# The last feature tile of a down projection, computed in two token ranges

## The chip, the cores and the metric

The kernel runs on one core of one Trainium2 chip. The metric is device time in microseconds (us) of one execution, lower is better. Three runs of the kernel before are known: 1992.32, 1992.97 and 1994.06 us, median 1992.97. Beside them there is a profile of one execution, which gives the start and duration of every instruction on the five engines: TensorE (PE; its weight loads are listed apart as PEld), VectorE (DVE), ScalarE (ACT), GpSimd (POOL) and SyncE (SP), which issues most transfers.

## The reference

One layer of a decoder trunk on 256 prompt tokens and 64 sample tokens (8 sequences of 8), model width 2048, in float32: a gated linear attention beside a causal pooling branch, merged by gates, projected and added to the residual; then a SwiGLU network of inner width 5632; then a last RMS norm. The change touches only the end:

```
gate, up = jnp.split(h2 @ w_gu, 2, axis=-1)
x = x + g2 * ((jax.nn.silu(gate) * up) @ w_down)
...
y_prompt = _rmsnorm(xp, final_norm_g)
y_sample = _rmsnorm(xs, final_norm_g)
```

The norm of a token needs the sum of squares over all 2048 features of that token. Different tokens do not depend on each other there.

## The kernel before

Activations lie with features on the 128 partitions and tokens along the free axis: `x1[k]` is feature tile k (16 tiles of 128 features) with T = 320 columns, 256 prompt tokens (TP) first, then 64 sample tokens (TS). Every large product is made in three passes of a rounded float32 type (fp32r): the weights are split into `hi` (a rounding copy, ScalarE, line 147) and `lo` (the rest, VectorE, line 148), the activations likewise, and `mm3` (lines 160 to 163) adds hi x hi, hi x lo and lo x hi into one PSUM bank. Each of these matmuls is preceded by a load of its 128 x 128 weights, also where two in a row use the same ones.

`proj` (line 165) computes two feature tiles at once. It loads chunks of four rows of weight tiles by 256 columns (512 KB, issued by SyncE, line 139), splits each in pairs, and runs 2 x 3 matmuls of 320 tokens for each of the two feature tiles per pair. `whi` and `wlo` have four buffers each (WB), the raw chunks five in two pools.

The SwiGLU inner width is handled in two halves of 22 tiles (`parts`). For each half the gate and up projections come first, then the down projection of that half over eight units `ui` of two feature tiles, added to `x1` by `residual` (lines 949 to 954). In the second half each finished feature tile k is also squared and added to `acc2` (lines 941 to 947), scaled by the norm's weight into `xg` (line 1052), transposed on TensorE in three pieces of 128 tokens (the helper `tr`, line 125), and copied from PSUM into the row tiles `yn[0..2]` (line 1058), which have tokens on partitions. The third row tile holds the 64 sample tokens alone, padded with zeros in `xg`.

After the last unit, the sums over features are made by matmuls of `acc2` with a column of ones (line 1066), then root and reciprocal (lines 1070 and 1071), and the six halves of the three row tiles are scaled, on VectorE for the first 1024 features (line 1078) and on ScalarE for the others (line 1080), and sent by SyncE (line 1082).

The order of instructions on each engine is written by a planner when the program is built: it runs a timeline of its own, takes whatever is ready in that timeline, and prefers what stands earlier in the program. At run time each engine keeps that order and waits by semaphores. PSUM accumulators come from a pool of two (`pm`), the small ones from a pool of four (`misc()`).

Of the kernel before, what the change touches and what calls it, by code (L numbers as in the profile page):

```python
# [79 lines left out]
def body(tc, A):  # L80
# [17 lines left out]
    def misc():  # L98
        return pmisc.tile([P, 512], F32, tag="m", name=nm("pm"))
# [23 lines left out]
    def tr(out, in_):  # L123
        k = in_.shape[0]
        PE.transpose(out, in_, ident[:k, :k])  # L125
# [815 lines left out]
    def sq_acc(acc, k, first):  # L941
        if first:
            S.activation(acc, x1[k], AF.Square)
        else:
            sq = fp.tile([P, T], F32, tag="sq", bufs=2, name=nm("sq"))
            S.activation(sq, x1[k], AF.Square)
            V.tensor_tensor(acc, acc, sq, op=ALU.add)
# [60 lines left out]


    acc2 = fp.tile([P, T], F32, tag="acc", name="acc2")  # L1010
    parts = ((0, 22), (22, 44))
    for pi, (f0, f1) in enumerate(parts):
        ah, al = {}, {}
# [21 lines left out]
        if pi == 0:  # L1035
            bcx.close()
        else:
            hcx.close()
            yp = ctx.enter_context(tc.tile_pool(name="yp", bufs=1, side="right"))
            yn = [yp.tile([P, D], F32, name="yn%d" % i) for i in range(3)]  # L1040
            xgs = [yp.tile([P, 3 * P], F32, name="xg%d" % i) for i in range(2)]
            for xg in xgs:
                G.memset(xg[:, T:3 * P], 0.0)
        for ui in range(8):
            ps = proj(wdn, 256 * ui, f0, f1, ah, al)
            for i in range(2):
                k = 2 * ui + i
                residual(ps, i, k, 5)
                if pi == 1:
                    sq_acc(acc2, k, k == 0)  # L1050
                    xg = xgs[k % 2]
                    S.activation(xg[:, 0:T], x1[k], AF.Copy, scale=FG[:, k:k + 1])
                    pt = misc()
                    for a in range(3):
                        tr(pt[:, a * P:(a + 1) * P], xg[:, a * P:(a + 1) * P])
                    for a in range(3):
                        n = P if a < 2 else TS
                        (S.copy if a == 0 else V.tensor_copy)(yn[a][:n, k * P:(k + 1) * P], pt[:n, a * P:(a + 1) * P])
            if pi == 1 and ui == 5:
                S.activation(tiny, acc2[:, 0:1], AF.Sqrt)  # L1060


    pt = misc()
    for a in range(3):
        n = P if a < 2 else TS
        PE.matmul(pt[:n, 2 * a:2 * a + 2], lhsT=acc2[:, a * P:a * P + n], rhs=ones[:, 0:2], start=True, stop=True)
    rr = fp.tile([P, 6], F32, name="rr")
    for a in range(3):
        n = P if a < 2 else TS
        S.activation(rr[:n, 2 * a:2 * a + 2], pt[:n, 2 * a:2 * a + 2], AF.Sqrt, scale=1.0 / D, bias=epst[:n])  # L1070
        V.reciprocal(rr[:n, 2 * a:2 * a + 2], rr[:n, 2 * a:2 * a + 2])
    ys = A["y_s"].rearrange("b t d -> (b t) d")
    for a in range(3):
        n = P if a < 2 else TS
        for c in range(2):
            sl = yn[a][:n, c * 1024:(c + 1) * 1024]
            if c == 0:
                V.tensor_scalar(sl, sl, rr[:n, 2 * a:2 * a + 1], None, op0=ALU.mult)
            else:
                S.activation(sl, sl, AF.Copy, scale=rr[:n, 2 * a:2 * a + 1])  # L1080
            dst = A["y_p"][0, a * P:(a + 1) * P] if a < 2 else ys
            nc.sync.dma_start(dst[:, c * 1024:(c + 1) * 1024], sl)
    ctx.close()


# [19 lines left out]
```

## Time and profile before

| what | us |
|---|---|
| median of three runs | 1992.97 (1992.32 to 1994.06) |
| span of the profiled execution, first to last instruction | 1989.4 |
| its last unit of the down projection (1953.6 to 1973.6) | 20.0 |
| from there to the end of the span | 15.8 |
| TensorE busy over the span | 1938.0 (97%) |

The time of an execution is taken around the whole program, the span from its first to its last instruction inside it; the profiled execution's own time is not listed apart from its span, and the median of the runs stands 3.6 us above that span. The page gives the busy time of each engine, 40 slices of the span, the transfers, the chain of work that ended last, and groups of equal instructions by line. Lines are those of the kernel before. A duration in a row is that of one instruction; instructions of one engine overlap in part, so the distance between two starts is the price of one in a stream.

### The profile page before, as it was taken

How to read it: one execution, taken by the hardware profiler on the slowest of the kernel's cores; microseconds unless marked ns; L12 is line 12 of the kernel's file. 1: busy time of each engine (PE TensorE's matmuls, PEld its weight loads, DVE VectorE, ACT ScalarE, POOL GpSimd, SP SyncE). 2: the span in 40 equal slices, each digit the busy share in tenths (PEclk: the TensorE clock that was granted, in tenths of full speed). 3: DMA queues.
4: the chain of work that ended last, by engine and by line, in shares of the span. 5: the costliest groups of instructions: out<-in, count | busy, mean ns of one | idle time of the engine just before them, and what ended most of it. 6: DMA issues, size and time to landing. Idle time of an engine off the chain costs nothing.

```text
span 1989.4 us, 34665 instructions
## 1 busy us (share of the span) xinstructions
PE 1938.0 (97%) x13808; PEld 1819.7 (91%) x13808; DVE 1002.8 (50%) x1918; ACT 829.4 (42%) x1483; POOL 179.3 (9%) x292
## 2 busy tenths in 40 slices
PE   5999999999999999999999999999999999999997
PEld 3778998889999889989979999999999999999997
DVE  2655645656356635665574444444444444444554
ACT  3323633544336433653344333433333434344443
POOL 1002101212121112111130000000000000000000
PEclk9999999999999999999999999999999999999998
DMA  9997458758975888479836555444444444444443
GB/s 316 344 333 239 141 170 281 231 182 288 302 221 171 274 283 257 148 248 329 265 100 197 185 185 178 156 147 145 150 148 154 149 151 151 152 150 140 149 141 101
DMA packets 309276, 400.59 MB, mean 201 GB/s; under 512 B 12418, under 2 KB 273058, under 8 KB 308778
## 3 DMA queue, kind: packets, MB, share of 16 engines
q1 hardware_dynamic: 279754, 291.17, 46.8%
q0 software_dynamic: 29360, 107.21, 15.6%
q8 instruction: 108, 1.77, 0.4%
q14 instruction: 54, 0.43, 0.1%
HBM read 373.90 MB, written 24.67 MB: 200 GB/s over the span
## 4 chain that ended last, share of the span: by engine, by line
PE 90%; DMA 6%; DVE 2%; ACT 1%; issue 0%; SPq 0%; POOL 0%; ACTq 0%; DVEq 0%
PE ps L161 26%; PE ps L163 26%; PE ps L162 26%; PE pm L281 3%; DMA araw<-w_ada 2%; DMA raw<-w_in 2%; PE pm L125 2%; PE pm L221 1%; DMA raw<-w_o 1%; PE pm L767 1%; PE pm L746 1%; PE pm L715 1%; DMA vr<-b_ada 1%; DVE wlo L148 1%; ACT whi L147 0%
## 5 line engine op out<-in xcount | busy, mean ns | idle before, releaser
L148 DVE TENSOR_TENSOR wlo<-raw,whi 128x512 fp32r<-128x512 f32 x952 | 654.9, 692 | 804.8 <-ACT whi L147 801.3
L147 ACT CAST whi<-raw 128x512 fp32r<-128x512 f32 x952 | 586.2, 622 | 923.3 <-PE ps L162 811.2
L161 PE MATMUL ps<-hh,whi 128*128 128x320 f32 x1408 | 443.1, 315 | 4.2 <-ACT whi L147 3.2
L162 PE MATMUL ps<-hl,whi 128*128 128x320 f32 x1408 | 439.2, 312 | 0.0
L163 PE MATMUL ps<-hh,wlo 128*128 128x320 f32 x1408 | 436.6, 312 | 1.3 <-DVE wlo L148 1.3
L161 PE MATMUL ps<-h2h,whi 128*128 128x320 f32 x1408 | 435.7, 310 | 0.0
L162 PE MATMUL ps<-h2l,whi 128*128 128x320 f32 x1408 | 435.5, 309 | 0.0
L163 PE MATMUL ps<-h2h,wlo 128*128 128x320 f32 x1408 | 435.4, 309 | 0.0
L161 PEld LDWEIGHTS ps<-hh,whi 128*128 128x128 f32 x1408 | 264.9, 188 | 28.2 <-issue 16.2
L163 PEld LDWEIGHTS ps<-hh,wlo 128*128 128x128 f32 x1408 | 264.2, 188 | 13.7 <-issue 7.3
L162 PEld LDWEIGHTS ps<-hl,whi 128*128 128x128 f32 x1408 | 265.1, 188 | 5.4 <-issue 4.6
L161 PEld LDWEIGHTS ps<-h2h,whi 128*128 128x128 f32 x1408 | 264.3, 188 | 3.4 <-ACT ah L317 3.4
L162 PEld LDWEIGHTS ps<-h2l,whi 128*128 128x128 f32 x1408 | 264.3, 188 | 0.0
L163 PEld LDWEIGHTS ps<-h2h,wlo 128*128 128x128 f32 x1408 | 264.3, 188 | 0.0
L161 PE MATMUL ps<-ah,whi 128*128 128x320 f32 x704 | 217.7, 309 | 0.0
L162 PE MATMUL ps<-al,whi 128*128 128x320 f32 x704 | 216.5, 308 | 0.0
L163 PE MATMUL ps<-ah,wlo 128*128 128x320 f32 x704 | 216.5, 308 | 0.0
L162 PEld LDWEIGHTS ps<-al,whi 128*128 128x128 f32 x704 | 132.0, 187 | 0.0
L161 PEld LDWEIGHTS ps<-ah,whi 128*128 128x128 f32 x704 | 131.9, 187 | 0.0
L163 PEld LDWEIGHTS ps<-ah,wlo 128*128 128x128 f32 x704 | 131.9, 187 | 0.0
L255 POOL DMA_DIRECT2D araw<-w_ada x64 | 54.9, 862 | 448.5 <-PE pm L281 419.2
L161 PE MATMUL ps<-mh,whi 128*128 128x320 f32 x256 | 79.5, 310 | 0.7 <-ACT whi L147 0.7
(280 smaller groups left out, 1609.4 us busy)
## 6 DMA issues: line engine op xcount, KB each, us to landing
raw<-w_gu SPq DMA_DIRECT2D x176, 512.0 KB, 3.5
raw<-w_in SPq DMA_DIRECT2D x173, 512.0 KB, 4.5
araw<-w_ada POOLq DMA_DIRECT2D x64, 1024.0 KB, 8.5
raw<-w_down SPq DMA_DIRECT2D x80, 512.0 KB, 3.5
raw<-w_ada SPq DMA_DIRECT2D x64, 512.0 KB, 6.6
S<-state_gla POOLq DMA_DIRECT2D x16, 1024.0 KB, 9.6
o_gs<-S POOLq DMA_DIRECT2D x16, 1024.0 KB, 5.9
raw<-w_o SPq DMA_DIRECT2D x32, 512.0 KB, 5.1
```

What stands on the lines that cost most here:

```text
L125: PE.transpose(out, in_, ident[:k, :k])
L147: S.copy(hi, raw)
L148: V.tensor_sub(lo, raw, hi.bitcast(F32))
L161: PE.matmul(ps, lhsT=whi, rhs=xhi, start=start, stop=False)
L162: PE.matmul(ps, lhsT=whi, rhs=xlo, start=False, stop=False)
L163: last_mm[:] = [PE.matmul(ps, lhsT=wlo, rhs=xhi, start=False, stop=stop).ins]
L221: PE.matmul(ps[32 * j:32 * j + 32, 0:w], lhsT=scT[:, k0 + i, :], rhs=raw[:, i, :], start=r == 0, stop=r == 3, tile_position=(0, 32 * j))
L255: nc.gpsimd.dma_start(t[:, r:r + step], wada[:, k0 + r:k0 + r + step, col:col + nb * P])
L281: PE.matmul(ps[32 * j:32 * j + 32, 0:w], lhsT=scT[:, k0 + r + j, :], rhs=ada_raw[n][:, r + j, :], start=k0 == 0 and first, stop=k0 + nk == ...
L715: PE.matmul(pt, lhsT=E["kdn"][:, s, d * P:(d + 1) * P], rhs=E["vn"][:, s], start=s == 0, stop=s == 1)
L746: PE.matmul(pt[32 * j:32 * j + 32, :], lhsT=qeP[:, d, 4 * gg + j, :], rhs=E["S0", gg, d][:, j], start=False, stop=d == 0, tile_position=(0 ...
L767: PE.matmul(pt, lhsT=E["kpn"][:, j, d * P:(d + 1) * P], rhs=E["vp"][:, gg], start=True, stop=True)
```

## The change

The last unit (feature tiles 14 and 15) is taken out of the loop for the second half. Its weights are loaded as before. Tile 14 is computed over all 320 tokens, while the split weights of tile 15 are kept in two new tiles (`wlast`, hi and lo). Tile 15 is then computed twice with them: for tokens 0 to 191, and for tokens 192 to 319 (TC = 192) in another PSUM tile. After each range its residual, squares, transposes and copies follow, and then `rows`, which makes the norms of that range's tokens, scales their rows and sends them.

The three windows of 128 tokens for transposes start at 0, 64 and 192 (WIN) and no longer at 0, 128 and 256; the middle one overlaps the first, and of it only its second half is sent. The third holds the last 64 prompt tokens and the 64 sample tokens. So there are eight output transfers, two of 128 rows and six of 64, where there were four of 128 rows and two of 64. The three row tiles become one tile, with one copy from PSUM per feature tile, on VectorE for even k and on ScalarE for odd k. The zero padding of `xg` goes.

```diff
 
 
     acc2 = fp.tile([P, T], F32, tag="acc", name="acc2")
+    TC = 192
+    WIN = (0, TC - P, TC)
+
+    def residual_part(acc, k, t0, t1):
+        e = min(t1, TP)
+        V.scalar_tensor_tensor(x1[k][:, t0:e], acc[:, t0:e], modp(5, k), x1[k][:, t0:e], op0=ALU.mult, op1=ALU.add)
+        if t1 > TP:
+            t = fp.tile([P, TS], F32, tag="rt", bufs=2, name=nm("rt"))
+            V.tensor_tensor(s3(t), s3(acc[:, TP:T]), mods(5, k), op=ALU.mult)
+            V.tensor_tensor(x1[k][:, TP:T], x1[k][:, TP:T], t, op=ALU.add)
+
+    def finish(k, t0, t1):
+
+        if k == 0:
+            S.activation(acc2, x1[k], AF.Square)
+        else:
+            sq = fp.tile([P, T], F32, tag="sq", bufs=2, name=nm("sq"))
+            S.activation(sq[:, t0:t1], x1[k][:, t0:t1], AF.Square)
+            V.tensor_tensor(acc2[:, t0:t1], acc2[:, t0:t1], sq[:, t0:t1], op=ALU.add)
+        xg = xgs[k % 2]
+        if t0 == 0:
+            S.activation(xg[:, t0:t1], x1[k][:, t0:t1], AF.Copy, scale=FG[:, k:k + 1])
+        else:
+            V.tensor_scalar(xg[:, t0:t1], x1[k][:, t0:t1], FG[:, k:k + 1], None, op0=ALU.mult)
+        pt = misc()
+        wins = [a for a in range(3) if t0 <= (TC if a == 2 else 0) and WIN[a] + P <= t1]
+        for a in wins:
+            tr(pt[:, a * P:(a + 1) * P], xg[:, WIN[a]:WIN[a] + P])
+        a, b = wins[0], wins[-1] + 1
+        (S.copy if k % 2 else V.tensor_copy)(yn[:, a:b, k * P:(k + 1) * P],
+                                             pt[:, a * P:b * P].rearrange("p (a t) -> p a t", t=P))
+
+    rr = fp.tile([P, 3, 2], F32, name="rr")
+    ys = A["y_s"].rearrange("b t d -> (b t) d")
+    yrows = ((A["y_p"][0, 0:P], 0, P, 0), (A["y_p"][0, P:TC], P - (TC - P), P, 1),
+             (A["y_p"][0, TC:TP], 0, TP - TC, 2), (ys, TP - TC, P, 2))
+
+    def rows(t0, t1):
+
+        a0, a1 = (0, 2) if t0 == 0 else (2, 3)
+        pt = misc()
+        for a in range(a0, a1):
+            PE.matmul(pt[:, 2 * a:2 * a + 2], lhsT=acc2[:, WIN[a]:WIN[a] + P], rhs=ones[:, 0:2], start=True, stop=True)
+        r = rr[:, a0:a1]
+        S.activation(r, pt[:, 2 * a0:2 * a1].rearrange("p (a t) -> p a t", t=2), AF.Sqrt, scale=1.0 / D, bias=epst)
+        V.reciprocal(r, r)
+        for a in range(a0, a1):
+            for c in range(2):
+                sl = yn[:, a, c * 1024:(c + 1) * 1024]
+                if c == 0:
+                    V.tensor_scalar(sl, sl, rr[:, a, 0:1], None, op0=ALU.mult)
+                else:
+                    S.activation(sl, sl, AF.Copy, scale=rr[:, a, 0:1])
+                for dst, p0, p1, aa in yrows:
+                    if aa == a:
+                        nc.sync.dma_start(dst[:, c * 1024:(c + 1) * 1024], yn[p0:p1, a, c * 1024:(c + 1) * 1024])
+
     parts = ((0, 22), (22, 44))
     for pi, (f0, f1) in enumerate(parts):
         ah, al = {}, {}
@@ -1037,49 +1094,51 @@
         else:
             hcx.close()
             yp = ctx.enter_context(tc.tile_pool(name="yp", bufs=1, side="right"))
-            yn = [yp.tile([P, D], F32, name="yn%d" % i) for i in range(3)]
-            xgs = [yp.tile([P, 3 * P], F32, name="xg%d" % i) for i in range(2)]
-            for xg in xgs:
-                G.memset(xg[:, T:3 * P], 0.0)
+            yn = yp.tile([P, 3, D], F32, name="yn")
+            xgs = [yp.tile([P, T], F32, name="xg%d" % i) for i in range(2)]
+            wlast = [yp.tile([P, f1 - f0, P], F32R, name="wlast%d" % i) for i in range(2)]
         for ui in range(8):
+            if pi == 1 and ui == 7:
+                break
             ps = proj(wdn, 256 * ui, f0, f1, ah, al)
             for i in range(2):
                 k = 2 * ui + i
                 residual(ps, i, k, 5)
                 if pi == 1:
-                    sq_acc(acc2, k, k == 0)
-                    xg = xgs[k % 2]
-                    S.activation(xg[:, 0:T], x1[k], AF.Copy, scale=FG[:, k:k + 1])
-                    pt = misc()
-                    for a in range(3):
-                        tr(pt[:, a * P:(a + 1) * P], xg[:, a * P:(a + 1) * P])
-                    for a in range(3):
-                        n = P if a < 2 else TS
-                        (S.copy if a == 0 else V.tensor_copy)(yn[a][:n, k * P:(k + 1) * P], pt[:n, a * P:(a + 1) * P])
+                    finish(k, 0, T)
             if pi == 1 and ui == 5:
                 S.activation(tiny, acc2[:, 0:1], AF.Sqrt)
 
-
-    pt = misc()
-    for a in range(3):
-        n = P if a < 2 else TS
-        PE.matmul(pt[:n, 2 * a:2 * a + 2], lhsT=acc2[:, a * P:a * P + n], rhs=ones[:, 0:2], start=True, stop=True)
-    rr = fp.tile([P, 6], F32, name="rr")
-    for a in range(3):
-        n = P if a < 2 else TS
-        S.activation(rr[:n, 2 * a:2 * a + 2], pt[:n, 2 * a:2 * a + 2], AF.Sqrt, scale=1.0 / D, bias=epst[:n])
-        V.reciprocal(rr[:n, 2 * a:2 * a + 2], rr[:n, 2 * a:2 * a + 2])
-    ys = A["y_s"].rearrange("b t d -> (b t) d")
-    for a in range(3):
-        n = P if a < 2 else TS
-        for c in range(2):
-            sl = yn[a][:n, c * 1024:(c + 1) * 1024]
-            if c == 0:
-                V.tensor_scalar(sl, sl, rr[:n, 2 * a:2 * a + 1], None, op0=ALU.mult)
-            else:
-                S.activation(sl, sl, AF.Copy, scale=rr[:n, 2 * a:2 * a + 1])
-            dst = A["y_p"][0, a * P:(a + 1) * P] if a < 2 else ys
-            nc.sync.dma_start(dst[:, c * 1024:(c + 1) * 1024], sl)
+    f0, f1 = parts[1]
+    ps = pmain.tile([P, 2, 512], F32, tag="pm", name=nm("ps"))
+    psb = pmain.tile([P, 2, 512], F32, tag="pm", name=nm("ps"))
+    wh, wl = wlast
+    for c0 in range(f0, f1, 4):
+        nk = min(4, f1 - c0)
+        raw = raw_chunk(wdn[:, c0:c0 + nk, 256 * 7:256 * 8], nk, 256)
+        for j in range(0, nk, 2):
+            hi = wp.tile([P, 2, 256], F32R, tag="whi", bufs=WB, name=nm("whi"))
+            lo = wp.tile([P, 2, 256], F32R, tag="wlo", bufs=WB, name=nm("wlo"))
+            src = raw[:, j:j + 2, 0:P]
+            S.copy(hi[:, :, 0:P], src)
+            V.tensor_sub(lo[:, :, 0:P], src, hi[:, :, 0:P].bitcast(F32))
+            q = c0 - f0 + j
+            src = raw[:, j:j + 2, P:2 * P]
+            S.copy(wh[:, q:q + 2], src)
+            V.tensor_sub(wl[:, q:q + 2], src, wh[:, q:q + 2].bitcast(F32))
+            for n in range(2):
+                kt = c0 + j + n
+                mm3(ps[:, 0, :T], hi[:, n, 0:P], lo[:, n, 0:P], ah[kt], al[kt], kt == f0, kt == f1 - 1)
+    residual(ps, 0, KT - 2, 5)
+    finish(KT - 2, 0, T)
+    for t0, t1 in ((0, TC), (TC, T)):
+        acc = ps[:, 1] if t0 == 0 else psb[:, 0]
+        for kt in range(f0, f1):
+            q = kt - f0
+            mm3(acc[:, t0:t1], wh[:, q], wl[:, q], ah[kt][:, t0:t1], al[kt][:, t0:t1], kt == f0, kt == f1 - 1)
+        residual_part(acc, KT - 1, t0, t1)
+        finish(KT - 1, t0, t1)
+        rows(t0, t1)
     ctx.close()
 
 
```

## The prediction

> **What bounds the kernel now.** I read the page first, then the last 36 us in two windows, then single instructions of the tail, and last the transfers.
>
> ```profile
> span 1989.4 us, 34665 instructions
> PE 1938.0 (97%) x13808; PEld 1819.7 (91%) x13808; DVE 1002.8 (50%) x1918; ACT 829.4 (42%) x1483; POOL 179.3 (9%) x292
> PE 90%; DMA 6%; DVE 2%; ACT 1%; issue 0%; SPq 0%; POOL 0%; ACTq 0%; DVEq 0%
> core 0: us, PE busy (x) PEld busy (x) DVE busy (x) ACT busy (x) POOL busy (x), PEclk, DMA share, GB/s
> 1953.60:1973.60 20.00, 20.00 (x139) 19.77 (x137) 8.71 (x20) 6.95 (x14) 0.00 (x0) 1.00 0.05 14
> 1973.60:1989.40 15.80, 1.69 (x13) 1.30 (x12) 5.70 (x18) 5.87 (x12) 0.00 (x0) 0.67 0.49 166
> ```
>
> TensorE is busy for 97% of the span and carries 90% of the chain that ended last. The first window is the last unit of the down projection (feature tiles 14 and 15): TensorE without a gap, at granted clock 1.00, VectorE under half busy, hardly a DMA. The second is the tail, 15.8 us in which TensorE works 1.69. The change shortens the second window and pays in the first, so two prices decide: a matmul of fewer tokens, and what the tail becomes.
>
> The tail in order (start, duration, engine, line):
>
> ```profile
> 1973.05 0.31 PE L161 MATMUL ps<-ah,whi 128*128 128x320 f32 x1
> 1973.34 0.30 PE L163 MATMUL ps<-ah,wlo 128*128 128x320 f32 x1
> 1973.68 0.48 DVE L950 SCALAR_TENSOR_TENSOR x<-ps,mod,x 128x256 f32<-128x256 f32 x1 [5.84 <-PE ps L163]
> 1974.08 0.21 DVE L953 TENSOR_TENSOR rt<-ps,mod 128x64 f32<-128x64 f32 x1
> 1977.90 0.55 ACT L1070 ACTIVATE rr<-pm,epst 128x2 f32<-128x2 f32 x3 [0.28 <-PE pm L1066]
> 1978.35 0.17 DVE L1071 RECIPROCAL rr<-rr 128x2 f32<-128x2 f32 x1
> 1978.43 0.73 DVE L1078 TENSOR_SCALAR yn<-yn,rr 128x1024 f32<-128x1024 f32 x1
> 1979.24 0.36 SPq L1082 DMA_DIRECT2D y_p<-yn  x1
> ```
>
> The last matmul starts at 1973.34, the first output transfer is issued at 1979.24 (5.90 us later), and the span ends at 1989.4: 16.06 us after that last start. Two matmul starts 0.29 apart over two steps give 0.147 us per matmul of 320 tokens. The remaining 10 us are transfers:
>
> ```profile
> GB/s 0 0 0 0 0 0 14 410 423 382 423 410 423 341 423 396 410 410 423 396 382 423 437 355 301 273 232 205 219 218 205 205 0 0 0 0 0 0 0 27
> y_p<-yn SPq DMA_DIRECT2D x4, 512.0 KB, 4.4
> y_s<-yn SPq DMA_DIRECT2D x2, 256.0 KB, 4.8
> 1980.10:1981.40 1.30, 0.00 (x0) 0.00 (x0) 0.45 (x1) 1.30 (x2) 0.00 (x0) 0.50 1.02 406
> ```
>
> The first row has 40 slices of 0.3 us from 1978.0. Data flow from 1980.10, 0.86 after the first issue; the four 128-row pieces run at about 405 GB/s, and once only 64-row pieces of y_s are left (the slices from 232 to the last 205) the rate is 214. Check: 2.1 MB at 405 and 0.52 MB at 214 take 5.18 + 2.45 = 7.63, so data end near 1987.73, and 1.67 us close the span.
>
> **The change part by part.** *Feature tile 15 in two ranges.* 66 matmuls of 320 tokens become 66 of 192 and 66 of 128. Every matmul still loads its own 128 weight columns, so the floor of that load counts:
>
> ```profile
> 810.03 0.23 PE L580 MATMUL pm<-cumr,w 128*128 128x128 f32 x1
> 810.09 0.27 PE L581 MATMUL pm<-cumr,w 128*128 128x128 f32 x1
> 810.03 0.30 PEld L581 LDWEIGHTS pm<-cumr,w 128*128 128x128 f32 x2
> 1977.05 0.53 PEld L1066 LDWEIGHTS pm<-cst,acc 128*128 128x128 f32 x4
> L163 PEld LDWEIGHTS ps<-hh,wlo 128*128 128x128 f32 x1408 | 264.2, 188 | 13.7 <-issue 7.3
> ```
>
> L580 and L581 are the only fp32r matmuls here with few moving columns. The 128-column one streams in 0.06 (810.03 to 810.09), so 0.46 ns per column as at 320; 192 would stream in 0.09. But weight loads follow one another no faster than 0.11: two span 0.30, one lasts 0.19; four span 0.53, (0.53 - 0.19)/3 = 0.113, there under matmuls of two columns. At 320 tokens that load hides under 0.147; at 192 and 128 it does not. I take 0.110 for both: 132 x 0.110 = 14.52 against 66 x 0.147 = 9.70, **+4.82 us**. Bounds: +0.1 if only streaming counted (66 x (0.09 + 0.06) = 9.9, with rounding 0.1 to 0.2 over the old), +5.2 at 0.113.
>
> [...]
>
> *Transposes and row sums inside the stream.* Three transposes of tile 14 and two of the first range, and four weight loads of its row sums, stood in the tail.
>
> ```profile
> 1959.48 0.31 PE L163 MATMUL ps<-ah,wlo 128*128 128x320 f32 x1
> 1959.62 0.49 PE L125 MATMUL pm<-cst,xg 128*128 128x128 f32 x3
> 1960.10 0.31 PE L162 MATMUL ps<-al,whi 128*128 128x320 f32 x1
> 1956.17 0.55 ACT L1052 ACTIVATE xg<-x,vec 128x320 f32<-128x320 f32 x1
> ```
>
> From 1959.48 to 1960.10 go two matmuls and three transposes: (0.62 - 0.29)/3 = 0.11 each. So 9 x 0.11 = **+0.99**. Queued behind them on TensorE are the second range's matmuls; they would wait if the inputs were late, but here xg is ready at 1956.72 and the transposes stand 2.9 us later in the order, so I cost that wait at nothing.
>
> *Tile 14 alone, splits for both.* TensorE now spends 0.88 per pair of rows of weights where it spent 1.76, while the same raw chunk is split into hi, lo and the kept weights of tile 15.
>
> ```profile
> L148 DVE TENSOR_TENSOR wlo<-raw,whi 128x512 fp32r<-128x512 f32 x93 | 64.3, 692 | 71.5 <-ACT whi L147 71.5
> L947 DVE TENSOR_TENSOR acc<-acc,sq 128x320 f32<-128x320 f32 x15 | 7.3, 490 | 1.8 <-ACT sq L946 1.2
> L946 ACT ACTIVATE sq<-x 128x320 f32<-128x320 f32 x15 | 6.9, 463 | 7.9 <-DVE x L954 7.9
> L1058 DVE COPY yn<-pm 128x128 f32<-128x128 f32 x16 | 4.7, 291 | 3.7 <-ACT yn L1058 3.6
> L1058 ACT COPY yn<-pm 128x128 f32<-128x128 f32 x16 | 4.2, 265 | 8.2 <-PE pm L125 8.2
> L1070 ACT ACTIVATE rr<-pm,epst 128x2 f32<-128x2 f32 x2 | 0.4, 260 | 0.3 <-PE pm L1066 0.3
> ACT whi L147 <- PE ps L162: 5.6, 5, 1.1
> 1955.43 0.37 SPq L139 DMA_DIRECT2D raw<-w_down  x1
> ```
>
> VectorE per pair: between 0.69 (one 512-wide operation) and 2 x 0.49 (320-wide rows). Eleven pairs are 7.6 to 10.8, plus 2 x (0.48 + 0.21 + 0.21 + 0.49) and a copy, some 3.3, for tiles 12 and 13, in 10.0 us of TensorE and with three pairs split ahead (ScalarE's cast waits for TensorE to free its buffers), worth 2.6. Stall: 0 to 1.5; I take 0, as two 256-wide halves lie nearer the one 512-wide row. The last raw transfer is issued 1.8 us into the unit, so loads are ahead. One 384-wide copy of output rows for three narrow ones, and the dropped zero fill on GpSimd, lie under TensorE's stream: nothing. Without that cover the copies count 0.27 + 2 x 0.29 now and at most some 0.5 (the 320-wide rows) then.
>
> *Rows of the first range during the second.* The second range holds TensorE 66 x 0.110 + 6 x 0.11 = 7.9 us. In it: residual (under 0.48), square (0.46), sum (0.49), row sums (0.7), root and reciprocal (0.26 + 0.17), scaling 0.73, with hand-overs: first issue 3.7 us after the first range ends, or 6.6 with the 2.9 us of lateness seen above. Its 128-row pieces (1.05 MB) need 2.6, its 64-row pieces (0.52 MB) 2.45. With 0.86 to the first data they end at 9.6 to 12.5, that is 1.7 to 4.6 us after the second range's last matmul.
>
> *What is left of the tail.* From the last matmul start: 0.30 to VectorE, three 64-wide operations 0.64, square at most 0.27, sum at most 0.29, row sums 0.5 (two loads and a matmul), root 0.26, reciprocal 0.17, scaling 0.73, issue 0.08: first issue at 3.24, data at 4.10. What they wait behind is at worst the first range's pieces until 4.6. Then 1.05 MB, now all in pieces of 64 rows, at 214 GB/s: 4.9; close 1.67. Sum 10.67 against 16.06: **-5.39**. Bounds: -7.8 if pieces of opposite partition halves shared the rate of 405 (2.6 for 4.9, less 0.1 for the second issue), -4.4 with 0.5 of waiting for the first range and 0.5 of longer hand-overs.
>
> [...]
>
> Sum: 4.82 + 0.99 + 0 - 5.39 = **+0.4 us**, 1989.8 against the span of 1989.4. The median of the runs, 1992.97, lies 3.6 above that span (launch and end outside it), which I keep: 1993.4.
>
> **The rivals.**
>
> *The weight load hides after all.* In a long stream of short matmuls the loads would overlap and streaming would set the pace. For it: the 0.06 between the two 128-column matmuls. Against: the loads around them stand 0.11 apart, and the four under two-column matmuls do too. Price: -4.7, so 1988.7; half hidden, 1991. [...] Chance 12 in 100, two thirds of it over 0.2% faster.
>
> *Opposite halves share the rate.* Only the last term moves: 1991.0. Chance 12; for it that the y_s pieces, on one half, ran at just half the rate of 405; against it that one queue feeds them in order.
>
> *Rows of the first range come too late (slower).* The order on TensorE is written by a planner. If the first range's row sums stand behind most of the second's matmuls, the pieces of both ranges drain after it. It decides from a first issue 6.1 us into the second range on: there 0.86 + 5.05 + 4.9 of data end just with the tail above. At the extreme, row sums behind the last matmul: 0.72 + 0.43 + 0.73 + 0.08 to the issue, 0.86, 9.95 of data, 1.67: 14.4, only 1.6 less than now; 4.82 + 0.99 - 1.6 = +4.2, 1997.2. For it: transposes stand 2.9 us late now, and cheap matmuls could let more of them slip ahead. Against: nothing else competes for VectorE and ScalarE there, so the chain is shorter than the one now. Chance 18.
>
> **How the numbers follow.** The sum above 58, hidden loads 12, shared rate 12, late rows 18. Its own range is 1991.5 to 1995.5 (stall, hand-overs, 0.113). To hold 8 in 10 I go to 1989.0 (fully hidden loads left out) and to 1997.2 (late rows at their extreme). A measurement of this kernel tells 0.2%, 4 us, from no change. Over 4 us faster: 8 of the hidden loads, 2 of the shared rate, 2 of the sum's own edge, 12. Over 4 us slower: 11 of the late rows, when a stall of tile 14 adds to them, 3 of the sum's own edge, 14. Within: 74.
>
> **What would show it.** In the profile after: matmuls of 192 and 128 tokens 0.11 apart, 14.5 us for both ranges (9.9 proves the first rival); no gap on TensorE in tile 14; the first output transfer issued 4 to 6.6 us after the first range's last matmul; 10.7 us from the last matmul start to the end; about 214 GB/s for the last pieces. The forecast is wrong if the last matmul starts less than 4 or more than 7.5 us later than 1973.34, or if the tail keeps over 12.5.

## The result, and the profile after

| | before | after |
|---|---|---|
| median of 12 runs, us | 1992.12 (1989.41 to 1994.38) | 1995.72 (1991.29 to 2000.45) |
| ratio after / before | | 1.0018, 95% interval 1.0009 to 1.0026 |
| span of the profiled execution, us | 1989.4 | 1996.0 (its own time 1998.04) |

The kernel is 3.6 us slower: inside the bound of 0.2% by a hair, inside the range (1989.0 to 1997.2), and 2.3 above the predicted 1993.4. Here are size, busy time and the engines' shares of the chain that ended last, of the kernel after:

```profile
span 1996.0 us, 34799 instructions
PE 1943.0 (97%) x13874; PEld 1826.0 (91%) x13874; DVE 1001.4 (50%) x1907; ACT 829.5 (42%) x1487; POOL 177.8 (9%) x290
PE 92%; DMA 4%; DVE 1%; ACT 1%; SPq 0%; issue 0%; POOL 0%; ACTq 0%; DVEq 0%
```

The two spans differ by 6.6 us, the medians by 3.6. Executions of one and the same kernel lie up to 5 us to either side of the medians in this table. In the profiled executions such differences arise early: from the first residual of the down projection's first half on, 525 us before the mark used next, all kernels here agree within 0.03 us until the planner's order begins to differ. So everything below is counted from one mark: the start of the residual of feature tile 6. It is this row before, and this one after (the timeline: start, duration, engine, line):

```profile
1893.60 0.48 DVE L950 SCALAR_TENSOR_TENSOR x<-ps,mod,x 128x256 f32<-128x256 f32 x1 [0.56 <-PE ps L163]
```

```profile
1896.53 0.48 DVE L950 SCALAR_TENSOR_TENSOR x<-ps,mod,x 128x256 f32<-128x256 f32 x1 [0.56 <-PE ps L163]
...
1959.32 0.22 PE L161 MATMUL ps<-ah,wlast 128*128 128x128 f32 x1
...
1968.58 0.31 PE L163 MATMUL ps<-ah,wlo 128*128 128x320 f32 x1
1968.72 0.22 PE L161 MATMUL ps<-ah,wlast 128*128 128x128 f32 x1
1968.92 0.48 DVE L950 SCALAR_TENSOR_TENSOR x<-ps,mod,x 128x256 f32<-128x256 f32 x1 [3.57 <-PE ps L163]
...
1971.46 0.27 PE L162 MATMUL ps<-al,wlast 128*128 128x128 f32 x1
1971.57 0.30 PE L161 MATMUL ps<-ah,wlast 128*128 128x192 f32 x1
...
1979.18 0.35 PE L163 MATMUL ps<-ah,wlast 128*128 128x192 f32 x2
1979.37 0.28 PE L161 MATMUL ps<-ah,wlast 128*128 128x128 f32 x1
...
1981.60 0.28 PE L163 MATMUL ps<-ah,wlast 128*128 128x128 f32 x1
...
1984.06 4.53 SPq L1066 DMA_DIRECT2D y_p<-yn  x5
```

By this mark the last matmul starts at 79.7 before and 85.1 after (+5.3), the end comes at 95.8 before and 99.45 after: **+3.7 us**, close to the 3.6 between the medians. The tail behind the last matmul start is 14.4 for 16.05.

The order of the matmuls in that fence is not the order of the program text. Behind the last 320-token matmul of tile 14 (1968.58) stand 26 matmuls of **128** tokens, the second range, from 1968.72 to 1971.46; only then does the first range (192 tokens) begin, 1971.57 to 1979.18; and when that is done, 2.4 us of the second range are left. 18 more of its matmuls stand inside tile 14, between 320-token ones (eleven in a row from 1959.32). So of the second range's 66 matmuls 44 run before the first range ends, and 22 behind it. The first output transfer is issued at 1984.06, 4.9 us after the first range's last matmul, and 2.5 after the last matmul of all.

Stage by stage (columns as in the prediction's windows; PEclk is the granted clock of TensorE as a share of its full speed):

```profile
core 0: us, PE busy (x) PEld busy (x) DVE busy (x) ACT busy (x) POOL busy (x), PEclk, DMA share, GB/s
1956.59:1971.50 14.91, 14.91 (x116) 14.89 (x114) 7.76 (x22) 6.34 (x16) 0.00 (x0) 1.00 0.06 19
1971.50:1979.20 7.70, 7.70 (x72) 7.70 (x71) 0.56 (x1) 0.00 (x0) 0.00 (x0) 1.00 0.00 0
1979.20:1981.65 2.45, 2.45 (x25) 2.45 (x23) 0.78 (x2) 0.71 (x2) 0.00 (x0) 1.00 0.00 0
1981.65:1996.00 14.35, 1.47 (x12) 1.16 (x10) 3.56 (x10) 4.49 (x8) 0.00 (x0) 0.60 0.59 184
```

The second row is the first range: VectorE 0.56 and ScalarE nothing in 7.7 us. The second range was to run behind the first and hide the first one's rows, but two thirds of it had been computed before. The third row is all that was left to hide the rows under. The transfers of the last stage, in 40 slices of 0.3 us from 1984.0:

```profile
GB/s 0 55 0 396 382 396 410 82 177 396 423 423 328 246 273 218 218 205 218 218 177 137 287 314 314 396 232 205 260 314 273 314 314 178 14 0 0 0 0 0
```

Data flow for 9.5 us where before they flowed for 7.8. Only the first pieces run at 400. The last seven full slices (232 to the second of the last two 314), where pieces on opposite partition halves alternate, have a mean of 273, above the 214 of one half alone.

### The profile page after: what moved, and what is told of

Its sections match the earlier page's. It is cut to its first block, busy times and chain, and to the rows that moved or that the text cites. A ratio compares the mean times of both kernels' runs of the same rounds, so it can differ in the third digit from the quotient of the medians.

```text
span 1996.0 us, 34799 instructions
## 1 busy us (share of the span) xinstructions
PE 1943.0 (97%) x13874; PEld 1826.0 (91%) x13874; DVE 1001.4 (50%) x1907; ACT 829.5 (42%) x1487; POOL 177.8 (9%) x290
## 4 chain that ended last, share of the span: by engine, by line
PE 92%; DMA 4%; DVE 1%; ACT 1%; SPq 0%; issue 0%; POOL 0%; ACTq 0%; DVEq 0%
PE ps L161 27%; PE ps L163 27%; PE ps L162 27%; PE pm L281 3%; PE pm L125 2%; PE pm L221 2%; DMA araw<-w_ada 1%; DMA raw<-w_o 1%; PE pm L767 1%; PE pm L746 1%; DMA vr<-b_ada 1%; PE pm L715 1%; DMA raw<-w_in 1%; DMA raw<-w_ada 0%; SPq L139 0%
## 5 line engine op out<-in xcount | busy, mean ns | idle before, releaser
L148 DVE TENSOR_TENSOR wlo<-raw,whi 128x512 fp32r<-128x512 f32 x941 | 646.5, 692 | 798.5 <-ACT whi L147 792.1
L147 ACT CAST whi<-raw 128x512 fp32r<-128x512 f32 x941 | 579.0, 622 | 911.2 <-PE ps L162 794.8
L161 PE MATMUL ps<-ah,whi 128*128 128x320 f32 x682 | 210.9, 309 | 0.0
L163 PE MATMUL ps<-ah,wlo 128*128 128x320 f32 x682 | 209.9, 308 | 0.0
L162 PE MATMUL ps<-al,whi 128*128 128x320 f32 x682 | 209.8, 308 | 0.0
L162 PEld LDWEIGHTS ps<-al,whi 128*128 128x128 f32 x682 | 127.8, 187 | 0.0
L161 PEld LDWEIGHTS ps<-ah,whi 128*128 128x128 f32 x682 | 127.8, 187 | 0.0
L163 PEld LDWEIGHTS ps<-ah,wlo 128*128 128x128 f32 x682 | 127.8, 187 | 0.0
L163 PE MATMUL ps<-mh,wlo 128*128 128x320 f32 x256 | 79.8, 312 | 0.2 <-DVE wlo L148 0.2
```

What stands on the lines that cost most here:

```text
L147: S.copy(hi, raw)
L148: V.tensor_sub(lo, raw, hi.bitcast(F32))
L161: PE.matmul(ps, lhsT=whi, rhs=xhi, start=start, stop=False)
L162: PE.matmul(ps, lhsT=whi, rhs=xlo, start=False, stop=False)
L163: last_mm[:] = [PE.matmul(ps, lhsT=wlo, rhs=xhi, start=False, stop=stop).ins]
```

## The experiments

All times in the table are from the profiled executions, one for each row, in us from the mark (residual of tile 6); "end" is the end of the span. Medians and ratios are of the timed runs against the kernel before on the same chip.

| kernel | last matmul starts | first issue | data | end | end against before | median; ratio (95%) |
|---|---|---|---|---|---|---|
| before | 79.7 | 85.6 | 86.5 to 94.3 | 95.8 | | |
| after | 85.1 | 87.5 | 88.4 to 97.8 | 99.45 | +3.7 | 1995.72; 1.0018 (1.0009 to 1.0026) |
| e1_swap | 85.7 | 83.4 | 84.3 to 94.5 | 96.1 | +0.3 | 1992.69; 1.0014 (1.0005 to 1.0024) |
| e2_hold | 86.7 | 84.4 | 85.2 to 95.6 | 97.2 | +1.4 | 1993.11; 1.0006 (0.9997 to 1.0016) |
| e3_one_range | 80.05 | 85.6 | 86.45 to 95.6 | 97.2 | +1.4 | 1992.26; 1.0004 (0.9995 to 1.0012) |
| e4_windows | 79.7 | 85.7 | 86.5 to 95.7 | 97.3 | +1.5 | 1991.70; 1.0005 (0.9997 to 1.0014) |
| e8_halves | 79.7 | 86.4 | 87.55 to 97.9 | 99.6 | +3.8 | 1996.72, one run |
| e7_rows_alone | 79.8 | 86.1 | 86.9 to 94.3 | 95.6 | -0.2 | 1990.16; 0.9994 (0.9986 to 1.0003) |
| e5_whole | 80.0 | 84.1 | 85.0 to 92.3 | 93.6 | -2.2 | 1988.89; 0.9981 (0.9972 to 0.9991) |
| e6_prompt_first | 90.2 | 84.9 | 85.8 to 97.2 | 98.5 | +2.7 | 1994.97; 1.0012 (1.0003 to 1.0021) |
| e6_again | 89.8 | 84.5 | 85.4 to 97.2 | 98.4 | +2.6 | 1993.32, one run |
| e9_wide | 86.1 | 84.0 | 84.9 to 92.8 | 94.1 | -1.7 | 1989.78, one run |

The table and the ratios say the same of after, e5 and e7. For e1 the ratio (+2.8 us, at least +1.0) is above the +0.3 of the table, and for e3 and e4 (+0.8 and +1.0) below it: differences of 1 us are not resolved by timed runs that spread over 5 or more, and the table is the closer look at the stage. Why e1's timed runs stand further from before than its profiled stage does is left open; by them alone after (+3.6) and e1 (+2.8) can't be told apart, and what is said below of their difference is a reading of the stage. How far the stage repeats is seen in e6_prompt_first and e6_again, one kernel twice: 0.4 us apart at the last matmul and 0.1 at the end.

### The order the prediction assumed, by another accumulator: e1_swap

The matmuls of the first range write into the second half of tile 14's PSUM tile, those of the second range into a PSUM tile of their own. Here they change places:

```diff
-        acc = ps[:, 1] if t0 == 0 else psb[:, 0]
+        acc = psb[:, 0] if t0 == 0 else ps[:, 1]
```

> The first range accumulates in the PSUM tile of its own and the second in the tile that feature tile 14 uses, the other way round than in the change; nothing else. In the order this gives, all 66 matmuls of the second range stand behind the first's, and the first's row sums after 31 of them. Theory A (the loss lies in the order: second-range matmuls pulled ahead of the first range, 22 of 66 left to hide the sending): last matmul as late as in the change, but the first output transfer is issued some 2.5 us before it instead of 2.4 us after it, the tail from the last matmul start falls from 14.4 us to between 9.3 and 10.7, and the time from 1995.7 to 1991.3 to 1992.4 us, that is 0.4 to 0.9 below the kernel before to 0.3 above it. Theory B (the loss lies in the eight transfers, six of them of 64 rows, whatever the order): the tail stays above 13 us and the time at 1994.5 or more.

The timeline of that kernel, then its transfers in 40 slices of 0.3 us from 1985.0:

```profile
1901.89 0.48 DVE L950 SCALAR_TENSOR_TENSOR x<-ps,mod,x 128x256 f32<-128x256 f32 x1 [0.56 <-PE ps L163]
...
1979.64 0.27 PE L163 MATMUL ps<-ah,wlast 128*128 128x192 f32 x1
1979.75 0.25 PE L161 MATMUL ps<-ah,wlast 128*128 128x128 f32 x1
...
1987.61 0.28 PE L163 MATMUL ps<-ah,wlast 128*128 128x128 f32 x1
...
1985.30 6.25 SPq L1066 DMA_DIRECT2D y_p<-yn  x5
```

```profile
GB/s 0 0 0 96 410 382 410 423 410 396 410 382 301 259 246 177 219 150 205 177 191 0 0 0 246 205 205 218 150 314 328 300 396 178 178 341 369 68 0 0
```

Now all 66 matmuls of the second range stand behind the first range's last one (1979.64), and the first output is issued at 1985.30, 2.3 us *before* the last matmul. The tail is 10.3 for the 10.67 of the sum, the last matmul starts 6.0 later than before for the 5.81, and the end is at +0.3 for the sum's +0.4. So the sum priced the order it assumed, and that order was not the one built; one accumulator's place is worth 3.4 us in the stage. In part the tail's agreement is luck: data of the second range begin 4.6 us after the last matmul start for the 4.1 of the sum, and take 4.2 us for its 4.9.

The three empty slices before the second group of pieces show that those do not wait for the first group: they wait for their own rows.

### The second range held back, accumulators as they were: e2_hold

```diff
+        hold = tc.issue_after(last_mm[0]) if t0 else nullcontext()
...
-            mm3(acc[:, t0:t1], wh[:, q], wl[:, q], ah[kt][:, t0:t1], ...)
+            with hold if kt == f0 else nullcontext():
+                mm3(acc[:, t0:t1], wh[:, q], wl[:, q], ah[kt][:, t0:t1], ...)
```

> The change with its PSUM tiles as they are, but the second range's matmuls are held behind the last of the first range in TensorE's order, so neither fills a gap while feature tile 14 is computed. Theory A: the same tail as with the swapped tiles (9.3 to 10.7 us). If the matmuls pulled ahead covered real gaps of TensorE (late splits in tile 14, or the wait of the first range for tile 14's residual, which reads the same PSUM tile), TensorE now shows them: up to 1 us at the residual and up to 1.5 us in tile 14, time 1992.5 to 1994.5. If they covered nothing: the time of the swapped tiles within 0.5 us. Theory B: 1994.5 or more.

```profile
1962.48 0.31 PE L163 MATMUL ps<-ah,wlo 128*128 128x320 f32 x1
1963.50 0.36 PE L161 MATMUL ps<-ah,wlast 128*128 128x192 f32 x1 [0.71 <-DVE rt L953]
...
1963.23 0.21 DVE L953 TENSOR_TENSOR rt<-ps,mod 128x64 f32<-128x64 f32 x1
```

With nothing pulled ahead, the first range does not follow tile 14 at once. It starts 1.02 us after tile 14's last matmul, and the row names who releases it: VectorE's L953, which *reads* tile 14 out of `ps`. Both accumulators are halves of one PSUM tile, and here writing the one waited for reading the other, 0.71 us by that row. This is the wait that the planner filled in the kernel after, with 26 matmuls (2.85 us) where 1.0 was to be filled. Why it took 26 isn't shown: that number comes from its own timeline.

Tile 14's last matmul starts at 70.05 here and at 72.05 after. The 18 second-range matmuls that stand inside tile 14 there cost 18 x 0.11 = 2.0, exactly that difference: they filled no gap. Holding is worth 2.2 of the 3.4 us, the free accumulator the other 1.15.

### The parts alone: e3_one_range, e4_windows, e8_halves

e3_one_range keeps the kept weights of tile 15 and the new rows, with a single range:

```diff
-        a0, a1 = (0, 2) if t0 == 0 else (2, 3)
+        a0, a1 = 0, 3
...
-    for t0, t1 in ((0, TC), (TC, T)):
-        acc = ps[:, 1] if t0 == 0 else psb[:, 0]
+    for t0, t1 in ((0, T),):
+        acc = psb[:, 0]
```

> The change without the ranges: feature tile 15 is computed once over all 320 tokens from its kept weights, after tile 14, and all rows are sent at the end, in the change's eight pieces. Price of the weight loads (0.110 to 0.113 us per matmul of 192 or 128 tokens against 0.147 for 320): last matmul 4.9 us earlier than in the change, 0.4 us later than in the kernel before (three transposes of tile 14 in the stream). The tail loses the work of tile 14, so the first issue comes 4.2 us after the last matmul start (5.9 in the kernel before). If pieces of 64 rows cost 1.2 us each whatever the partition half, data take 9.9 us and the time is 1993.1; if pieces on opposite halves share the full rate in part, as the last 3 us of the changed kernel suggest (about 300 GB/s), 1991.7.

e4_windows is the loop of before to its end, with only the rows of after: one row tile, one copy per tile, windows at 0, 64 and 192, eight pieces.

```diff
-            if pi == 1 and ui == 7:
-                break
...
-    f0, f1 = parts[1]
-    ps = pmain.tile([P, 2, 512], F32, tag="pm", name=nm("ps"))
...
-        rows(t0, t1)
+    rows(0, T)
```

> The kernel before with only the change's other part: one row tile with one copy per feature tile, windows of tokens at 0, 64 and 192, and eight transfers, two of 128 rows and six of 64; both feature tiles of the last unit together, no ranges. The matmul stream is that of the kernel before. If every piece of 64 rows costs 1.2 us: data take 9.9 us for 7.6, time +2.3, 1994.4. If opposite halves share: 2.6 + 2.45 + 3.5 = 8.6, +0.9, 1993.0. If the number of pieces does not matter: 1992.1. The single copy is expected to be worth nothing, as it lies under TensorE's stream.

Its transfers, in 40 slices of 0.3 us from 1978.0:

```profile
GB/s 0 0 0 96 423 369 410 437 396 382 423 355 341 246 232 164 219 205 191 150 205 219 328 328 341 355 150 150 259 355 396 260 205 150 0 0 0 0 0 0
```

The matmuls end and the first output is issued as before; only the data take longer, 9.2 us for 7.8. So **the eight pieces cost 1.4 us by themselves**, and with what follows them the end is at +1.5. That lies between the two prices expected, 9.9 and 8.6 us of data. Neither one copy per tile nor the missing zero fill moves anything else. In after and e1 this price is paid as well.

e3 moves the end by the same +1.4. Its tail has a second price, though. The windows around its transposes and row sums:

```profile
1972.40:1974.50 2.10, 0.23 (x2) 0.00 (x0) 1.26 (x4) 0.92 (x2) 0.00 (x0) 1.00 0.00 0
1974.50:1976.50 2.00, 1.93 (x9) 1.84 (x9) 0.07 (x1) 0.48 (x2) 0.00 (x0) 0.54 0.00 0
```

The clock falls to 0.50 at 1974.65, and three transposes and six row sums fill 1.93 us, 0.21 each instead of 0.11: 0.95 lost. The first issue comes 5.55 after the last matmul start; without that it would be at about 4.6, so tile 14 finished early is worth 1.3 of before's 5.9. The last section says when this happens.

e8_halves takes before and sends each 128-row piece as two of 64 rows:

```diff
-            nc.sync.dma_start(dst[:, c * 1024:(c + 1) * 1024], sl)
+            for p0 in range(0, n, 64):
+                nc.sync.dma_start(dst[p0:p0 + 64, c * 1024:(c + 1) * 1024], sl[p0:p0 + 64])
```

> The kernel before with each 128-row output transfer cut into two of 64 rows, one per partition half, issued one behind the other; ten transfers of 64 rows in all. If transfers on opposite halves serialize at the rate of one half (214 GB/s), data take 12.2 us for 7.8; if two in flight share the full rate, 7.8 as before; the changed kernel's last 3 us, where halves alternate at about 300 GB/s, suggest about 9.5.

Its transfers, in 40 slices of 0.3 us from 1982.0:

```profile
GB/s 0 0 186 208 197 175 295 306 371 262 164 295 361 284 284 131 295 339 306 251 186 284 339 350 317 273 251 164 109 11 0 0 0 0 0 22 0 0 22 0
```

Ten 64-row pieces, halves alternating for the first eight, move 2.62 MB in 10.3 us: 254 GB/s. Full serialization at 214 would take 12.2, a shared rate with the y_s pieces alone 7.6 or so. The truth lies nearer to serialization. Of the end's +3.8, 2.5 are in the data and 0.8 ahead of the first issue, where the clock fell to 0.50 (at 1977.89) among the transposes. (One run, without an interval.)

### Rows that are sent whole: e7_rows_alone, e5_whole

Since the price of the eight pieces does not depend on the ranges, other rows were tried. The two prompt row tiles go as four pieces of 128 rows as before. The sample rows are laid out as 128 partitions by 1024 (features 0 to 1023 on partitions 0 to 63, the others above), so one VectorE operation scales them, and they go last in two pieces. For tile 15, the prompt's residual, squares, transposes, sums, scaling and sending come before the samples'.

```diff
-            yn = yp.tile([P, 3, D], F32, name="yn")
+            yn = yp.tile([P, 2, D], F32, name="yn")
+            yq = yp.tile([P, D // 2], F32, name="yq")
...
+            if a == 2:
+                V.tensor_scalar(yq, yq, rr[:, 2, 0:1], None, op0=ALU.mult)
+                for h in range(2):
+                    nc.sync.dma_start(ys[:, h * 1024:(h + 1) * 1024], yq[TS * h:TS * h + TS, :])
+                continue
...
-        for kt in range(f0, f1):
-            q = kt - f0
-            mm3(acc[:, t0:t1], wh[:, q], wl[:, q], ah[kt][:, t0:t1], ...)
+    acc = psb[:, 0]
+    for kt in range(f0, f1):
+        q = kt - f0
+        mm3(acc[:, 0:T], wh[:, q], wl[:, q], ah[kt], al[kt], kt == f0, kt == f1 - 1)
+    for t0, t1 in ((0, TP), (TP, T)):
```

That is e5_whole: tile 14 first, tile 15 with kept weights in *one* range of 320 tokens, then the two groups of tokens in turn. e7_rows_alone has the same rows at the end of before's unchanged loop.

> Feature tile 14 first, then tile 15 once over all 320 tokens from its kept weights (no ranges); windows of tokens at 0 and 128 again, so the prompt rows go in four transfers of 128 rows; of the sample rows the first 1024 features lie on partitions 0 to 63 and the others on 64 to 127, two transfers of 64 rows on opposite halves; after the last matmul the prompt tokens are finished before the sample tokens. Measured from the same instruction in every trace (the residual of an earlier feature tile): last matmul 0.3 us later than in the kernel before, as in the run with one range; first output transfer 3.8 to 4.5 us after the last matmul start (5.9 before), 5 to 5.5 if the clock of TensorE falls to half before the transposes as in the run with one range; data 6.9 us (7.8 before); end 1.3 to 2.5 us earlier than in the kernel before. If the tail were set by what stands around the transfers and not by them, no gain.

> The kernel before with only the new rows of the run with tile 15 whole: both feature tiles of the last unit together, no kept weights, but sample rows on both partition halves and, for tile 15, prompt tokens finished before sample tokens. Last matmul as in the kernel before; first issue 5.0 to 5.6 us after it (5.9 before), data 6.9 us for 7.8; end 0.8 to 1.8 us earlier than in the kernel before. What the run with tile 15 whole gains beyond this is the worth of moving tile 14 out of the tail (about 1 us expected).

e5's timeline, and its transfers in 40 slices of 0.3 us from 1978.0:

```profile
1895.06 0.48 DVE L950 SCALAR_TENSOR_TENSOR x<-ps,mod,x 128x256 f32<-128x256 f32 x1 [0.56 <-PE ps L163]
...
1975.02 0.32 PE L163 MATMUL ps<-ah,wlast 128*128 128x320 f32 x1
1975.18 0.27 PE L125 MATMUL pm<-cst,xg 128*128 128x128 f32 x1
1976.77 0.44 PE L125 MATMUL pm<-cst,xg 128*128 128x128 f32 x2 [1.32 <-ACT xg L1036]
...
1979.17 2.90 SPq L1078 DMA_DIRECT2D y_p<-yn  x4
```

```profile
GB/s 0 0 0 0 0 0 150 382 423 396 396 423 396 410 396 410 382 410 410 369 437 423 410 369 301 246 177 150 260 410 205 0 0 0 0 0 0 0 0 0
```

e5 beats both kernels: 1988.89 us, ratio 0.9981 to before (0.9972 to 0.9991), and -2.2 by the table. Its last matmul starts only 0.24 later than before, since 320-token matmuls keep their price: 0.146 us each in e5 (six starts, 1974.29 to 1975.02), 0.147 before. The first issue comes 4.15 after the last matmul start for before's 5.9, since tile 14 is finished and transposed while tile 15 runs, and only the prompt's rows stand before it. Its data take 7.4, where 6.9 were expected. In this execution the clock fell behind the transposes, at 1977.98; had it fallen before them, as in e3, some 1 us of the gain would be missing. The rows alone (e7) give nothing that can be told from before, where 0.8 to 1.8 us were expected. e7's transposes and row sums fell into the half clock, as in e3 (four transposes in 0.91 us, from 1973.27 to 1974.18), so its first issue is late by some 1 us that it need not have lost.

### Two ranges with these rows: e6_prompt_first, e9_wide

```diff
-    for t0, t1 in ((0, TC), (TC, T)):
-        acc = ps[:, 1] if t0 == 0 else psb[:, 0]
+    for t0, t1 in ((0, TP), (TP, T)):
+        acc = psb[:, 0] if t0 == 0 else ps[:, 1]
```

> Two ranges as in the change, but 256 prompt tokens first and the 64 sample tokens second, the first in the PSUM tile of its own and the second in that of tile 14, rows and transfers as in the run with tile 15 whole. All 66 matmuls of 64 tokens stand behind those of 256. If the load of 128 weight columns sets a floor of 0.11 us per matmul, the second range takes 7.3 us although its columns stream in 0.03 us each, and the last matmul comes 5.4 to 6.0 us later than in the kernel before; if the floor followed the tokens, 1 to 2 us later. The prompt rows (2.1 MB, 5.2 us at 405 GB/s) go out under the second range: first issue 5 to 6 us after the first range ends; after the last matmul only the sample's 0.5 MB are left. End 0.5 to 2.5 us earlier than in the kernel before with the floor, over 5 us earlier without it.

The order came out as wanted: 66 matmuls of 256 tokens, then 66 of 64. The last matmul nevertheless starts at 90.2, 4.7 us later than a price of 0.11 gives, and the end is at +2.7, where a gain of 0.5 to 2.5 was expected. Two windows of the second range:

```profile
1973.90:1977.10 3.20, 3.20 (x32) 3.20 (x31) 0.91 (x2) 1.08 (x3) 0.00 (x0) 1.00 0.00 0
1977.20:1985.80 8.60, 8.60 (x43) 8.60 (x42) 1.59 (x3) 2.82 (x4) 0.00 (x0) 0.50 0.48 187
```

TensorE is busy throughout, by the profile, and the granted clock falls to 0.50 in the middle of the stream: 32 instructions in 3.2 us, then 43 in 8.6. To see whether the width does it, e9_wide computes tokens 192 to 319 in the second range, 64 of them a second time for nobody, and the kernel above ran once more beside it as e6_again.

```diff
+            m0 = T - P if t0 else 0
-            mm3(acc[:, t0:t1], wh[:, q], wl[:, q], ah[kt][:, t0:t1], ...)
+            mm3(acc[:, m0:t1], wh[:, q], wl[:, q], ah[kt][:, m0:t1], ...)
```

> The two ranges of the prompt-first kernel, 256 and 64 tokens, with one change: the second range's matmuls take tokens 192 to 319, 128 wide instead of 64 (the 64 additional columns repeat prompt tokens and nobody reads them). In the kernel with 64-token matmuls the pitch was 0.111 us at first, and the granted clock fell to 0.50 3.3 us after that stream began, with TensorE never idle. Theory (the clock follows how much of the time columns stream, not whether instructions stand in the queue): 128-token matmuls take the same 0.11 us each, so the stream keeps clock 1.00 to its end, the second range takes 7.3 us instead of 12.06, and the last matmul starts about 4.7 us earlier, some 85.5 us after the first residual of tile 6 in place of 90.2; the end comes near 94 to 95 after it, for 98.5. Rival (the fall belongs to this order of work, to a wait in it or to the chip's state, not to the width): the clock falls again about 3 us into the second range, and the last matmul starts near 90.

> The prompt-first kernel with 64-token matmuls once more, unchanged, beside the one with 128-token matmuls. If its fall of the clock belongs to the narrow stream: granted clock 0.50 again from about 3 us into the second range, last matmul about 90 us after the first residual of tile 6. If it was a mishap of one execution: clock 1.00 through the range and the last matmul near 85.5.

Windows of e6_again, then those of e9_wide:

```profile
1971.40:1975.00 3.60, 3.60 (x36) 3.60 (x34) 0.91 (x2) 1.08 (x3) 0.00 (x0) 1.00 0.00 0
1975.10:1982.90 7.80, 7.80 (x39) 7.80 (x39) 1.59 (x3) 2.82 (x4) 0.00 (x0) 0.50 0.58 231
```

```profile
1971.80:1975.50 3.70, 3.70 (x36) 3.70 (x35) 0.91 (x2) 1.08 (x3) 0.00 (x0) 1.00 0.00 0
1975.50:1979.60 4.10, 4.10 (x39) 4.10 (x39) 1.59 (x3) 2.80 (x4) 0.00 (x0) 1.00 0.30 121
```

The fall repeats with 64 columns (last matmul at 89.8) and does not occur with 128, where the same 39 instructions take 4.1 us instead of 7.8 and the last matmul starts at 86.1. Twice the columns made the range 3.7 us shorter. The order of the matmuls on TensorE is the same in the three traces, all 628 from the mark on, so the order is not the cause. e9's end is at -1.7 (one execution): two ranges seem to win with rows that are sent whole, though not more than one range does (e5, -2.2).

## Why the prediction came out as it did

The time lies inside the stated range, and that is luck as far as the sum goes: 1995.72 is above the sum's own range (1991.5 to 1995.5) and fits only because room had been left for late rows. By the signs that the prediction names, it was wrong: the tail keeps 14.4 us, and over 12.5 was to show that. The last pieces run at a mean of 273 GB/s and not at 214.

**The time outside the span.** Own time less span is 2.04 us in the profiled execution after and 1.8 to 2.7 in the experiments' ones, not 3.6. By that the profiled execution of before took some 1991.4, a quick one, and the rest is spread between executions. The forecast of the difference is untouched.

**Feature tile 15 in two ranges, +4.82.** Confirmed. In the fences of after, matmuls stand 0.11 apart at 192 tokens (1971.57 to 1979.18) and at 128 (1968.72 to 1971.46); e6's 64 tokens cost the same at full clock. So at 64, 128 and 192 tokens the price did not follow the tokens; it is the pitch of the weight loads in the rows of before (0.11, and 0.113 under matmuls of two columns), and the rival that the load hides is dead.

**Transposes and row sums inside the stream, +0.99.** Of the nine only the three transposes of tile 14 went there; the first range's two and its four row-sum loads stayed behind the last matmul, 0.66 less. With 192 tokens at 0.113 rather than 0.110 (0.2 more), the last matmul moved by 5.34 and not by 5.81.

**Tile 14's stall, 0.** Right: the first window of after has TensorE busy for 14.91 of 14.91 us. But the forecast "no gap on TensorE in tile 14" was met partly by matmuls of the second range, which I had not expected there and which cost 2.0.

**Rows of the first range during the second.** This is the step that failed. It says "The second range holds TensorE 66 x 0.110 + 6 x 0.11 = 7.9 us", all of it behind the first range. Behind the first range it held TensorE for 2.4. The chain itself was right: from the first range's end to the first issue 4.9 us passed, within the 3.7 to 6.6 given. What there was to hide it under was gone. I had read the program's text as TensorE's order, although I had written that the planner takes whatever is ready. The second range's accumulator was a free PSUM tile and the first's was not: e2's row (L953 releases the first 192-token matmul) shows the wait of 1.02 us, and e1, which only swaps the accumulators, moves the end from +3.7 to +0.3 in the stage.

**What is left of the tail, -5.39.** It measured -1.67 in after. In e1, where the order is the assumed one, the tail is 10.3 for the forecast's 10.67. The 4.9 us of data in that sum take the 214 GB/s of one half for pieces on both halves, an estimate that no run shows: such pieces moved at a mean of 273 in after's last slices and at 254 in e8, its y_s pieces included.

**The rivals.** "Rows of the first range come too late" had its extreme at a tail of 14.4 and +4.2; measured were 14.4 and +3.7. The tails agree because two errors cancel: the first issue came 2.5 us after the last matmul for 1.96, and the data took 9.46 for 9.95. I gave it 18 in 100, and this is what happened, by another road: I looked for row sums that slip back, and for a competitor on VectorE and ScalarE; in the event the matmuls behind which they should have hidden slipped forward. "Opposite halves share the rate" is a fraction of the way there: e8 moves 254 GB/s, where 214 was one half and 405 all rows. The sum had priced the eight pieces at 9.95 us of data; in e4 they take 9.2, still 1.4 more than the six pieces of before.

So after's +3.7 is: last matmul +5.3; first issue after it 5.9 to 2.5, -3.4; data 7.8 to 9.5, +1.65; close +0.1.

## What to carry to other kernels

Where a planner writes the order, a later piece of work with a free buffer can overtake an earlier one that waits, as 44 of 66 matmuls did here, and the overlap is lost with no gap to be seen: look in the order at what stands between the producer and the work that was to hide its consumer. In e2 an accumulator waited for the reader of the other one in its PSUM tile, and 1.02 us passed between two matmuls. Before splitting a matmul by columns, price the pieces by measured ones (here 0.11 us at 64, 128 and 192 columns, 0.147 at 320), and the output by the rate of its pieces (here 405 GB/s for 128 rows, 214 for 64 rows on one half): the best kernel here (e5) does without the split. Of its 2.2 us, 1.3 can be put down to finishing one feature tile earlier (by e3's rows) and the rest to the rows; that division is worked out and was not tested by a run of its own.

## What the runs showed of the hardware

**In e6 a narrow stream of matmuls lost the clock although TensorE never waited.** The clock changes in these traces stand on a grid of 3.41 us: the last stretch at 1.00 is 952.32 us long in some executions, 955.73 and 959.14 in others (279, 280 and 281 times 3.413), and the short stretches at 0.50 earlier in the span are 3.41 or 6.83 (3.41 from 1019.71 in before, 6.83 from 373.52 in after). Start, length (us) and granted clock of the last stretches, from the trace's clock records:

```
before           1023.13 955.73 1.0    1978.86 12.55 0.5
e3_one_range     1022.33 952.32 1.0    1974.65 17.16 0.5
e6_prompt_first  1024.81 952.32 1.0    1977.13 19.14 0.5
e9_wide          1022.55 959.14 1.0    1981.70  8.32 0.5
```

In these traces the falls at the end of the kernels stand at the end of a grid interval in which columns streamed for a small part of the time. With 0.46 ns per column (0.147 us for 320), a stream of 64 columns every 0.11 us streams for 27% of the time, and in both e6 and e6_again the clock fell at the end of the first interval that lay in it (1977.13, but for the interval's first 0.1 us, and 1975.08); at 128 columns it is 54%, and e9 kept 1.00. Behind the last matmul it was the same: an interval filled to 43% by 320-token matmuls (before, 1972.03 to 1975.45) kept the clock for the next one, one filled to 36% (e3, 1971.24 to 1974.65) lost it. So, but for the 64-token kernels, the fall came 2.1 to 5.5 us after the last matmul start, by where the grid lay, and decided whether a tail's transposes cost 0.11 or 0.21: in e3, e7 and e8 it came before or among them, in before (1978.86), after (1984.61) and e5 (1977.98) behind them.

Counted in the same way over whole traces (0.46 ns for each column of every matmul), the 7 falls in before and after stand behind intervals filled to 34% or less, and the 1128 intervals after which the clock stayed at 1.00 were filled to 43% or more. Over all twelve traces the 44 falls stand behind 38% or less; of the 6761 intervals after which the clock stayed only seven were filled to so little, each of them the first interval after the clock had risen, within the first 41 us of the span. These runs show a fall in an instruction stream without any idle time: in e6 TensorE is busy for 3.20 of 3.20 us ahead of it and for 8.60 of 8.60 behind it. That the share of streaming columns decides was not shown: only the comparison of 64 with 128 columns was made to test it, and something else that grows with the columns would fit as well.

**Pieces on opposite partition halves moved a little faster than pieces on one half.** e8's 254 GB/s, the two y_s pieces on one half included, are 19% above the 214 of one half alone, and after's last slices reach 314. The 128-row pieces moved at 405, and with 64-row pieces in place of some (e4) or all of them (e8) the end came 1.5 and 3.8 us later than in before.
